# Moving the matmul operands of a hybrid decoder layer to other places in SBUF, modulo 512 bytes

## The chip, the core and the metric

The kernel runs on one core of one Trainium2 chip. The metric is the device time of one execution in microseconds (us); the kernel before takes 1278.26 us, the median of three runs between 1277.83 and 1278.36.

Five engines matter here: PE (TensorE, matrix products; its weight loads are a stream of their own, PEld), DVE (VectorE), ACT (ScalarE), POOL (GpSimd) and SP, which issues nearly all the transfers. A matmul has a stationary operand of 128x128 (the weights, loaded first) and a moving operand that is streamed past it; the sum lands in PSUM. SBUF is the on-chip memory from which both are read, and what is changed is where in it some of these operands lie.

## The reference

One decoder layer on 1024 tokens plus 16 meta tokens of width 1024, all in float32:

```python
h = layer_norm(concat([meta, x]), in_ln_g, in_ln_b)
z = h @ w_in + b_in                                  # 1024 -> 3840
q, k, v, c_in, gates = split(z)
y_attn = swa_sink_attention(q, k, v, sinks, rel_bias) @ w_attn_proj
c = c_val * sigmoid(c_gate)                          # c_in in two halves
c = silu(layer_norm(causal_dwconv(c, 31 taps)))
y_conv = c @ w_conv_proj
mixed = sigmoid(g_attn) * y_attn + sigmoid(g_conv) * y_conv
h = layer_norm(ALPHA * h + mixed @ w_out, ln1_g, ln1_b)
up = causal_dwconv(h @ ffn_w_up, 3 taps)             # 1024 -> 2 * 2816
u, g = split(up)
f = (gelu(g) * u) @ ffn_w_down                       # 2816 -> 1024
out = layer_norm(ALPHA * h + f, ln2_g, ln2_b)[:, 16:]
```

## The kernel before

Every float32 operand of a product is split into a rounded high part and the remainder (`hi`, `lo`), and a product is three matmuls: high by high, high by low, low by high. The stages follow each other on PE: input projection (z), attention, the two branch projections with the gates, the output projection, then the feed-forward layer as two large products, `up` (line 1476) and `down` (line 1609), which are more than half of the time.

**Up.** Both large products are done by a scheme with seven block products in place of eight (sums of blocks are formed beforehand, results are combined afterwards). The layer's normalised rows are turned and stored as four blocks; seven sums or blocks of them (`B11, B21, BT2, BT1, BT3, BT4, B22`), each with its `hi` and `lo`, stay in SBUF for the whole product. They are held twice, once for each half of the tokens: sub 0 has 258 columns, sub 1 has 256. `B_AT[sub][q]` gives tile and column at which each lies. These are the moving operands. The stationary ones are blocks of the weights, in a ring of ten places (`RING`): four at the start of `RHO`, four in the buffers `whi`/`wlo` (called `ws` there), two more in `RHO` from column 6160. Weight block number n (seven for each of the 22 chunks c, in the order B11, B21, BT4, BT2, BT1, BT3, B22) goes to place n modulo 10.

For each chunk c, `prod` runs seven products in the order B11, B21, BT2, BT4, BT1, BT3, B22; each is twelve matmuls on sub 0 and then twelve on sub 1 with the same weights. That makes 154 products of twelve on each half. Within a product on sub 1 all twelve moving operands begin at the same address modulo 512 bytes, since 256 columns are 1024 bytes; on sub 0 they step by 8 bytes with k and by 32 between `hi` and `lo`. Behind PE, DVE and ACT combine the seven results, apply the three-tap convolution and the gelu, and split the weights that come next; SP loads the weights, stores the results and loads them again for `down`.

**Down.** `operand` loads 42 pairs of operands, splits them, and puts the i-th pair at `F_AT[i % 6]` (results of `up`, the stationary side here) and at `W_DN[i % 7]` (weights, the moving side, 512 columns). Five pairs in six have two rows of blocks and give 24 matmuls, the sixth has one and gives 12; the first pair of the second product is prepared ahead of the last one of the first. In all 924 matmuls.

**Where the tiles lie.** SBUF is given out by pools, from the left (low addresses up) and from the right (high addresses down), without gaps. The bytes per partition at which the tiles begin are, with the remainder modulo 512 in brackets: `whi`/`wlo`/`ws` 12736, 16832, 20928 and 25024 (448 each), `RHC` 53696 (448), `RHO` 86976 (448), `OA` 136672 (480), `RX` 187808 (416), `OC` 196064 (480). Columns have 4 bytes. `RHO` from column 6160 is therefore at 0, so that two of the ten ring places (8 and 9) are at 0 and the other eight at 448. The sums on sub 0 are at 448, 448, 480, 32, 96, 160, 416 in the order of `B_AT[0]`, on sub 1 four at 480 (`OC`) and three at 448 (`RHC`).

Besides these, `OC` holds the convolution branch and `OA` the attention branch as moving operands of the branch projections (tile `ps_p`), and `OA` (four of eight), `RX` and `RW` hold the weights, moving there, of the output projection (tile `ps_w`, lines 295 to 300). The order of the work is written out by hand for PE and in large part for DVE (`after` adds an order without a wait), the rest is left to a planner with ranks; a tile waits for those that held its bytes before.

Of the kernel before, what the change touches and what calls it, by code (L numbers as in the profile page):

```python
# [23 lines left out]
F = mybir.dt.float32  # L24
R = mybir.dt.float32r
# [4 lines left out]
P = 128  # L30
# [71 lines left out]
def tile_hybrid_layer(  # L102
# [41 lines left out]
    RHC = arena.tile([P, 8320], R, name="RHC")  # L144
    RHO = arena.tile([P, 8320], R, name="RHO")
# [745 lines left out]
    with rank(RK_EVAC):  # L891
# [8 lines left out]


    late = ctx.enter_context(tc.tile_pool(name="late", bufs=1, side="right", reuse_waits="tile"))
    OC = late.tile([P, 8320], R, name="OC")
    oa_stack = ExitStack()
    OA = oa_stack.enter_context(tc.tile_pool(name="oa", bufs=1, side="left", reuse_waits="tile")).tile(
        [P, 8320], R, name="OA")
    tmp_stack = ExitStack()
    tmp_p = tmp_stack.enter_context(tc.tile_pool(name="tmp", bufs=1, side="right", reuse_waits="tile"))

# [4 lines left out]
    def conv(c, hl, a, b):  # L914
        o = (c * 2 + hl) * T
        return OC[:, o + a:o + b]

    def pin(ins):

        if pinned:  # L920
            after(ins, pinned[-1])
        pinned.append(ins)
# [9 lines left out]
    def cln_var(g):  # L932
# [8 lines left out]

        hi, lo = (OC[:, i * T + a:i * T + b] for i in (2, 3))
        pin(dve.tensor_copy(hi, s_))
# [29 lines left out]
    def oo(r, hl, a, b):  # L973
        o = (r * 2 + hl) * T
        return OA[:, o + a:o + b]

# [38 lines left out]
    RX = rx_p.tile([P, 2064], R, name="RX")  # L1015
# [25 lines left out]
    def prep_wo(k, raw=None, behind=None):  # L1041
        if k < 4:
            hi, lo = OA[:, k * 2048:k * 2048 + 1024], OA[:, k * 2048 + 1024:k * 2048 + 2048]
        elif k < 6:
# [85 lines left out]
    def quadrant(sub, kk, h):  # L1130
        i = h * KC + kk * 4
        return FA[:, h1_at(sub, i):h1_at(sub, i + 4)]

    B_AT = [[(RHC, 6144), (RHO, 4096), (OA, 0), (OA, 2064), (OA, 4128), (OA, 6192), (RX, 0)],
            [(OC, 0), (OC, 2048), (OC, 4096), (OC, 6144), (RHC, 0), (RHC, 2048), (RHC, 4096)]]
    B11, B21, BT2, BT1, BT3, BT4, B22 = range(7)

    def bsum(sub, q, hl):
        n = SUB[sub][1] - SUB[sub][0]
        t, o = B_AT[sub][q]  # L1140
        return t[:, o + hl * 4 * n:o + (hl + 1) * 4 * n]
# [401 lines left out]
    T1, T3, T4, T2 = (blk(td, 0, 2048, q * 512) for q in range(4))  # L1543
    S2, S3, S4, S1 = (blk(sd, 0, 2048, q * 512) for q in range(4))

    F_AT = [(RHC, 6144), (RX, 0), (RHC, 2048), (RHO, 0), (RHO, 2048), (RHO, 4096)]
    W_DN = [(OC, 0), (OC, 2048), (OC, 4096), (OC, 6144), (RHC, 0), (RHC, 4096), (RHO, 6144)]

    RXFs = [RXF[:, 0:1024], RXF[:, 1024:2048]]
    FAs = [FA[:, i * 1024:(i + 1) * 1024] for i in range(6)]  # L1550
# [7 lines left out]
    def operand(i, src, j, n, raws, places):  # L1558
        raw = raws[i % len(raws)]
        if raw is None:  # L1560
            raw = wraw([P, D])
        raw = raw[:, :n * 512]
        ins = load(raw.rearrange("p (n c) -> p n c", c=512), src(j, n))
        after(ins, loads[-1] if loads else f_stores[-5])
        loads.append(ins)
        t, o = places[i % len(places)]
        hi, lo = (t[:, o + x:o + x + n * 512] for x in (0, 1024))
        nc.scalar.copy(hi, raw)
        los.append(nc.vector.tensor_tensor(lo, raw, f32(hi), OP.subtract))
        if len(los) > 1:  # L1570
            after(los[-1], evacs.pop() if evacs else los[-2])
        return hi, lo

    def down_operands():
# [4 lines left out]
        for i, (f, w, j, n) in enumerate(x):  # L1579
            yield (n,) + operand(i, f, j, n, F_RAW, F_AT) + operand(i, w, j, n, W_RAW, W_DN)  # L1580

# [181 lines left out]
```

## Time and profile before

| | |
|---|---|
| median of 3 runs | 1278.26 us (1277.83 to 1278.36) |
| the profiled execution | 1278.45 us |
| its span, first to last instruction | 1276.2 us |
| PE busy | 1265.2 us, 99% |
| PEld busy | 1192.4 us, 93% |
| DVE busy | 1084.1 us, 85% |
| ACT busy | 588.0 us, 46% |
| mean granted TensorE clock | 0.999 |
| up, line 1476 | from 612.3 to 1054.7 us of the span, 3696 matmuls |
| down, line 1609 | from 1054.7 to 1268.2 us, 924 matmuls |

The profile is one execution. Matmuls are pipelined: the record of one reaches past the start of the next, so that its length (280 ns for 256 columns in `up`) says little about the rate. The rate is read in the timeline, from the start of a row to the start of the row after it; a row there stands for a run of like matmuls, with its start, its length, the line, and the tiles as output<-moving,stationary. Tiles are named without numbers of buffers, so that `RHO` as weights can be any ring place in it; which one it is follows from the number of the weight block.

### The profile page before, as it was taken

The numbers are of one execution on the slowest core, as the hardware profiler recorded it, in microseconds if no ns is written. First come the engines' busy times: TensorE is split into PE (matmuls) and PEld (weight loads), VectorE is DVE, ScalarE is ACT, GpSimd is POOL, SyncE is SP. The second block draws the span as 40 slices with busy tenths as digits, with TensorE's granted clock in tenths as the row PEclk, the third lists the DMA queues.
The fourth block names the chain that finished last, engine by engine and source line by source line (L and its number), as shares of the span: only waits on it lengthen the run. The fifth ranks groups of instructions, "written<-read, shape, count | busy, mean of one in ns | idle before, by whom it ended". The sixth has DMA issues, their size and how long they took to land.

```text
span 1276.2 us, 21682 instructions
## 1 busy us (share of the span) xinstructions
PE 1265.2 (99%) x8546; PEld 1192.4 (93%) x8546; DVE 1084.1 (85%) x1837; ACT 588.0 (46%) x1066; POOL 53.0 (4%) x28
## 2 busy tenths in 40 slices
PE   9999999999999999999999999999999999999997
PEld 8999999999999999788899999999999998888886
DVE  7899989999998577548899898988989877995697
ACT  7523245645483223344755455455454544544330
POOL 0000000010112231000000000000000000000000
PEclk9999999999999999999999999999999999999999
DMA  7294633332256554222155545454454567998722
GB/s 275 73 306 108 181 94 100 100 95 88 67 149 191 156 150 117 83 99 81 53 169 195 185 176 201 163 202 149 157 191 161 200 226 280 389 328 297 247 83 83
DMA packets 96152, 212.10 MB, mean 166 GB/s; under 512 B 10787, under 2 KB 35939, under 8 KB 95922
## 3 DMA queue, kind: packets, MB, share of 16 engines
q1 hardware_dynamic: 84282, 199.64, 47.0%
q10 hardware_dynamic: 11768, 11.08, 2.7%
q8 instruction: 67, 1.10, 0.4%
q14 instruction: 35, 0.29, 0.1%
HBM read 150.29 MB, written 62.70 MB: 167 GB/s over the span
## 4 chain that ended last, share of the span: by engine, by line
PE 97%; DVE 1%; DMA 1%; ACT 0%; issue 0%; SPq 0%; DVEq 0%
PE px L1476 15%; PE py L1476 10%; PE ps_x L1609 9%; PE ps_z L299 8%; PE ps_z L295 8%; PE ps_z L300 8%; PE ps_z L1609 7%; PE pz L1476 5%; PE pw L1476 5%; PE ps_p L299 2%; PE ps_p L300 2%; PE ps_p L295 2%; PE ps_w L295 2%; PE ps_w L300 2%; PE ps_w L299 2%; PE ps_z L511 2%
## 5 line engine op out<-in xcount | busy, mean ns | idle before, releaser
L663 DVE SCALAR_TENSOR_TENSOR FA<-cin,cols,FA 128x1026 f32<-128x1026 f32 x120 | 155.1, 1304 | 0.2
L299 PE MATMUL ps_z<-RHC,whi 128*128 128x384 f32 (+2 forms) x324 | 104.7, 323 | 0.0
L295 PE MATMUL ps_z<-RHO,whi 128*128 128x384 f32 (+2 forms) x324 | 104.7, 323 | 0.0
L299 PE MATMUL ps_z<-RHO,whi 128*128 128x384 f32 (+2 forms) x324 | 104.0, 321 | 0.0
L295 PE MATMUL ps_z<-RHC,whi 128*128 128x384 f32 (+2 forms) x324 | 103.9, 321 | 0.0
L300 PE MATMUL ps_z<-RHC,wlo 128*128 128x384 f32 (+2 forms) x324 | 103.6, 320 | 0.0
L300 PE MATMUL ps_z<-RHO,wlo 128*128 128x384 f32 (+2 forms) x324 | 103.3, 319 | 0.0
L1298 DVE TENSOR_TENSOR RHO<-wr,RHO 128x512 fp32r<-128x512 f32 x94 | 63.4, 684 | 10.9 <-ACT RHO L1297 10.9
L1297 ACT CAST RHO<-wr 128x512 fp32r<-128x512 f32 x94 | 56.6, 619 | 21.3 <-DVE wr L1315 9.9
L266 ACT CAST whi<-wr 128x1024 fp32r<-128x1024 f32 x37 | 38.9, 1052 | 56.8 <-PE ps_z L299 34.3
L295 PEld LDWEIGHTS ps_z<-RHO,whi 128*128 128x128 f32 x324 | 60.9, 188 | 0.5 <-issue 0.3
L299 PEld LDWEIGHTS ps_z<-RHC,whi 128*128 128x128 f32 x324 | 60.9, 188 | 0.4
L300 PEld LDWEIGHTS ps_z<-RHC,wlo 128*128 128x128 f32 x324 | 61.0, 188 | 0.2
L300 PEld LDWEIGHTS ps_z<-RHO,wlo 128*128 128x128 f32 x324 | 60.9, 188 | 0.1
L295 PEld LDWEIGHTS ps_z<-RHC,whi 128*128 128x128 f32 x324 | 60.8, 188 | 0.2
L299 PEld LDWEIGHTS ps_z<-RHO,whi 128*128 128x128 f32 x324 | 60.9, 188 | 0.1
L1315 DVE TENSOR_TENSOR wr<-wr 128x512 f32<-128x512 f32 x88 | 60.0, 682 | 0.2
L1488 ACT COPY FA<-px 128x514 f32<-128x514 f32 (+2 forms) x23 | 13.1, 571 | 82.0 <-PE px L1476 82.0
L269 POOL TENSOR_TENSOR wlo<-wr,whi 128x1024 fp32r<-128x1024 f32 x17 | 41.3, 2429 | 187.4 <-ACT whi L266 168.9
L670 ACT ACTIVATE FA<-ps_z,cols 128x386 f32<-128x386 f32 (+2 forms) x48 | 26.0, 541 | 46.7 <-PE ps_z L300 42.2
L1298 DVE TENSOR_TENSOR ws<-wr,ws 128x512 fp32r<-128x512 f32 x60 | 40.6, 684 | 6.1 <-ACT ws L1297 6.0
L1476 PE MATMUL px<-OA,RHO 128*128 128x258 f32 x324 | 43.5, 283 | 0.0
(467 smaller groups left out, 3589.1 us busy)
## 6 DMA issues: line engine op xcount, KB each, us to landing
wr<-in_w_up_dram SPq DMA_DIRECT2D x44, 512.0 KB, 4.3
wr<-in_w_z_dram SPq DMA_DIRECT2D x30, 512.0 KB, 3.6
fd<-FA SPq DMA_DIRECT2D x44, 256.0 KB, 2.4
OB<-in_w_down_dram SPq DMA_DIRECT2D x19, 512.0 KB, 5.8
qt<-qd SPq DMA_DIRECT2D x28, 256.0 KB, 3.8
td<-OB SPq DMA_DIRECT2D x12, 512.0 KB, 3.2
sums<-fd SPq DMA_DIRECT2D x12, 512.0 KB
sd<-sums SPq DMA_DIRECT2D x12, 512.0 KB, 2.8
```

The costliest lines, as they stand in the source:

```text
L266: ins = nc.scalar.copy(hi, raw)
L269: return (nc.vector if quick else nc.gpsimd).tensor_tensor(lo, raw, f32(hi), OP.subtract)
L295: ins = nc.tensor.matmul(ps, ah, bh, start=i == 0, stop=False)
L299: nc.tensor.matmul(ps, ah, bl, start=False, stop=False)
L300: last = nc.tensor.matmul(ps, al, bh, start=False, stop=i == n - 1)
L663: nc.vector.scalar_tensor_tensor(acc[c], cin[:, j:j + U], wc, acc[c], OP.mult, OP.add)
L670: nc.scalar.activation(t, ps, AF.Tanh, bias=bcol(14 + i), scale=0.5)
L1297: nc.scalar.copy(hi, src)
L1298: ins = nc.vector.tensor_tensor(lo, src, f32(hi), OP.subtract)
L1315: ins = nc.vector.tensor_tensor(*x)
L1476: ins = nc.tensor.matmul(o, x[:, ks], bmat(sub, q, hl, k), start=first and k + j == 0, stop=k == 3 and j == 2, skip_group_check=not first)
L1609: nc.tensor.matmul(banks[i], l[:, ts], r[:, ws], start=first and a and x + k == 0, stop=z and x == len(ops) - 1 and k == 2, skip_group_che ...
```

## The change

Two small tiles that nothing reads or writes are added: 96 bytes in the pool of `OC`, 32 bytes in front of `OA`. `OC` comes to lie 96 bytes lower, at 195968 (384 modulo 512), and with it all that is given out below it on the right: `RX` to 187712 (320), `RW`, the raw and sum buffers of `down`. `OA` goes to 136704 (0). In `RHC` the operands of `up` and of `down` begin 112 columns, 448 bytes, later, which is 384 modulo 512. The sums on sub 0 come to 384, 448, 0, 64, 128, 192, 320, on sub 1 all seven to 384. In `down` the stationary side is at 384, 320, 384, 448, 448, 448, and the moving side at 384 six times and at 448 once. No instruction is added, removed or resized; the weights of `up` stay where they are.

```diff
     late = ctx.enter_context(tc.tile_pool(name="late", bufs=1, side="right", reuse_waits="tile"))
+
     OC = late.tile([P, 8320], R, name="OC")
+    late.tile([P, 24], F, name="pad_c")
     oa_stack = ExitStack()
-    OA = oa_stack.enter_context(tc.tile_pool(name="oa", bufs=1, side="left", reuse_waits="tile")).tile(
-        [P, 8320], R, name="OA")
+    oa_p = oa_stack.enter_context(tc.tile_pool(name="oa", bufs=1, side="left", reuse_waits="tile"))
+    oa_p.tile([P, 8], F, name="pad_a")
+    OA = oa_p.tile([P, 8320], R, name="OA")
...
-    B_AT = [[(RHC, 6144), (RHO, 4096), (OA, 0), (OA, 2064), (OA, 4128), (OA, 6192), (RX, 0)],
-            [(OC, 0), (OC, 2048), (OC, 4096), (OC, 6144), (RHC, 0), (RHC, 2048), (RHC, 4096)]]
+    B_AT = [[(RHC, 6256), (RHO, 4096), (OA, 0), (OA, 2064), (OA, 4128), (OA, 6192), (RX, 0)],
+            [(OC, 0), (OC, 2048), (OC, 4096), (OC, 6144), (RHC, 112), (RHC, 2160), (RHC, 4208)]]
...
-    F_AT = [(RHC, 6144), (RX, 0), (RHC, 2048), (RHO, 0), (RHO, 2048), (RHO, 4096)]
-    W_DN = [(OC, 0), (OC, 2048), (OC, 4096), (OC, 6144), (RHC, 0), (RHC, 4096), (RHO, 6144)]
+    F_AT = [(RHC, 6256), (RX, 0), (RHC, 2160), (RHO, 0), (RHO, 2048), (RHO, 4096)]
+    W_DN = [(OC, 0), (OC, 2048), (OC, 4096), (OC, 6144), (RHC, 112), (RHC, 4208), (RHO, 6144)]
```

## The prediction

> **What bounds the kernel now.** I read the page's first part, the chain, PE's waits, a table by stage, and then PE's timeline.
>
> ```profile
> PE 1265.2 (99%) x8546; PEld 1192.4 (93%) x8546; DVE 1084.1 (85%) x1837; ACT 588.0 (46%) x1066; POOL 53.0 (4%) x28
> PE 97%; DVE 1%; DMA 1%; ACT 0%; issue 0%; SPq 0%; DVEq 0%
> ```
>
> PE is the chain: 97% of the span hangs on it. So any nanosecond taken from or added to a matmul reaches the end, if nothing else becomes late.
>
> ```profile
> engine line waited for: us in total, times, longest us
> PE pw L1476 <- ACT FA L1278: 0.9, 1, 0.9
> PE px L1476 <- ACT OB L1488: 0.4, 1, 0.4
> ...
> core 0: us, PE busy (x) PEld busy (x) DVE busy (x) ACT busy (x) POOL busy (x), PEclk, DMA share, GB/s
> 740.00:850.00 110.00, 110.00 (x930) 110.00 (x929) 101.63 (x163) 55.17 (x93) 0.00 (x0) 1.00 0.52 182
> 1054.70:1150.00 95.30, 95.30 (x415) 77.29 (x414) 82.06 (x103) 42.85 (x45) 0.00 (x0) 1.00 0.92 332
> ```
>
> PE waits for nobody worth naming, and its clock is full (1.00). In `up` DVE is busy 101.63 of 110 us, 92%: a cover that would be gone if PE got more than 8% faster. In the first half of `down` the transfers are at 0.92 of the DMA engines; that one I come back to.
>
> What is left to change is thus how long one matmul takes. Rows of `up` on PE, from chunks 4, 7 and 8 (start, length, line, output<-moving,weights; I take start to start):
>
> ```profile
> 698.31 1.60 PE L1476 MATMUL pz<-RHO 128*128 128x258 f32 x12
> 699.75 1.58 PE L1476 MATMUL pz<-OC,RHO 128*128 128x256 f32 x12
> ...
> 761.06 1.60 PE L1476 MATMUL px<-OA,RHO 128*128 128x258 f32 x12
> 762.50 1.57 PE L1476 MATMUL px<-OC,RHO 128*128 128x256 f32 x12
> 763.90 1.61 PE L1476 MATMUL pw<-OA,RHO 128*128 128x258 f32 x12
> 765.35 1.59 PE L1476 MATMUL pw<-RHC,RHO 128*128 128x256 f32 x12
> 766.77 1.60 PE L1476 MATMUL py<-OA,RHO 128*128 128x258 f32 x12
> ...
> 773.92 1.59 PE L1476 MATMUL py<-RHC,ws 128*128 128x256 f32 x12
> 775.35 1.60 PE L1476 MATMUL px<-RHC,ws 128*128 128x258 f32 x12
> 776.79 1.57 PE L1476 MATMUL px<-OC,ws 128*128 128x256 f32 x12
> 778.20 1.59 PE L1476 MATMUL pz<-RHO,ws 128*128 128x258 f32 x12
> 779.62 1.57 PE L1476 MATMUL pz<-OC,ws 128*128 128x256 f32 x12
> 781.03 1.62 PE L1476 MATMUL px<-OA,RHO 128*128 128x258 f32 x12
> 782.49 1.58 PE L1476 MATMUL px<-OC,RHO 128*128 128x256 f32 x12
> 783.91 1.60 PE L1476 MATMUL pw<-OA,RHO 128*128 128x258 f32 x12
> 785.35 1.53 PE L1476 MATMUL pw<-RHC,RHO 128*128 128x256 f32 x12
> 786.71 1.61 PE L1476 MATMUL py<-OA,RHO 128*128 128x258 f32 x12
> ```
>
> The row to see is 785.35 against 765.35: the same product one chunk later, the same moving tile `RHC` at 448 modulo 512, 256 columns, twelve matmuls. One takes 1.42 us (765.35 to 766.77), the other 1.36 (785.35 to 786.71). The difference is the ring place of the weights: block 7x8+2 = 58 is in place 8, at 0 modulo 512, so that the moving operand lies 64 bytes below its weights; block 51 is in place 1, at 448, the same address. I call moving minus weights the distance d. On sub 1 the trace thus has: d = 0, 1.42 to 1.43 (765.35, 773.92); d = +32 (`OC` on 448), 1.40 to 1.41 (762.50, 776.79, 779.62); d = -32 (`OC` on place 9, block 59), 1.42 (782.49); d = -64, 1.36. The change puts all seven sums of sub 1 at 384, which is d = -64 for eight ring places of ten and d = -128 for two.
>
> **The change part by part.** Nothing is issued more or less, no queue is passed, and no wait is added in the code: the sums in `RHC` now straddle two of its old rows of `mixed`, but the last of these to be read, for the row tile before the first of the sums, is the same one as before. So the cost is in the rates alone.
>
> *Sub 1 of `up`.* Of 154 products 30 have their weights in places 8 and 9 (n modulo 10): 17 with `OC`, 13 with `RHC`. The other 124 go to d = -64: 71 from `OC` at 1.405 and 53 from `RHC` at 1.425. I take 1.365 for each, the row at 785.35 with half a hundredth for its rounding: 71 x 0.04 + 53 x 0.06 = 6.0 us less. The 30 go to d = -128, which the trace doesn't show; bounds 1.36 and 1.43, the fastest and slowest sub 1 rows. Now they take 17 x 1.42 + 13 x 1.36 = 41.8; at the bounds 40.8 or 42.9, so -1.0 to +1.1. Nothing puts it nearer to either; I take the middle, 0.
>
> *Sub 0 of `up`.* Here the distance steps within a product and the rows differ less: `OA` 1.44, 1.45, 1.46, 1.44 (761.06, 763.90, 781.03, 783.91), `RHC` 1.44 (775.35), `RHO` 1.42 and 1.44 (778.20, 698.31). `OA` is at odd multiples of 32 from the weights, `RHC` and `RHO` at a multiple of 64, and `OA` goes to multiples of 64. 132 products move (all but `RHO`'s 22): between 0.02 less and 0.02 more each, -2.6 to +2.6. The even rows are on average 0.014 below the odd ones, which over 88 `OA` products would be 1.2; with so few rows I take -0.5.
>
> *`down`.* Its rows, 24 matmuls of 512 columns each:
>
> ```profile
> 1054.67 5.76 PE L1609 MATMUL ps_z<-OC,RHC 128*128 128x512 f32 x24
> 1060.27 5.66 PE L1609 MATMUL ps_z<-OC,RX 128*128 128x512 f32 x24
> 1065.78 5.76 PE L1609 MATMUL ps_z<-OC,RHC 128*128 128x512 f32 x24
> ...
> 1076.97 5.63 PE L1609 MATMUL ps_z<-RHC,RHO 128*128 128x512 f32 x24
> 1082.44 2.88 PE L1609 MATMUL ps_z<-RHO,RHC 128*128 128x512 f32 x12
> 1085.16 5.61 PE L1609 MATMUL ps_x<-RHC,RHO 128*128 128x512 f32 x24
> 1090.61 5.65 PE L1609 MATMUL ps_x<-OC,RX 128*128 128x512 f32 x24
> ...
> 1115.65 5.61 PE L1609 MATMUL ps_z<-RHC 128*128 128x512 f32 x24
> 1121.09 5.75 PE L1609 MATMUL ps_z<-RHO,RX 128*128 128x512 f32 x24
> 1126.69 5.77 PE L1609 MATMUL ps_z<-OC,RHC 128*128 128x512 f32 x24
> ```
>
> d = +32 takes 5.60 (1054.67, 1121.09), d = +64 5.51 (1060.27), d = 0 5.44 to 5.47 (1115.65, 1076.97, 1085.16), say 5.45. Walking i through `F_AT[i % 6]` and `W_DN[i % 7]` gives, in units of 24 matmuls: before, 21 at +32, 13.5 at 0, 4 at +64, in sum 117.6 + 73.6 + 22.0 = 213.2 us (the stage is 213.5). After: 14.5 at 0, 7.5 at +64, 1 at +128, and 15.5 at d = -64, which 512 columns don't show. Its bounds: 5.60, the slowest row, and 5.33, which is d = 0 less what the same step saves on 256 columns (0.06 on twelve). d = 0 and d = +64, the nearest multiples of 64, stand at 5.45 and 5.51; I take 5.50. After: 79.0 + 41.3 + 5.5 + 85.3 = 211.1, so -2.1, with bounds -4.8 and -0.6.
>
> *Output and branch projections.*
>
> ```profile
> 534.86 0.40 PE L295 MATMUL ps_w<-OA,RHC 128*128 128x512 f32 x1
> ...
> 536.96 0.40 PE L295 MATMUL ps_w<-OA,RHC 128*128 128x512 f32 x1
> ```
>
> Nine matmuls with `OA` take 2.10 us, 233 ns each, as `down`'s d = +32. Four of eight weight rows are in `OA`; 192 matmuls (8 row tiles x 2 halves x 4 x 3) go from +32 to +64, 5.60 to 5.51 on 24: -0.7. `RX` and `RW` go from -32 to -128, and the branch projections' 768 matmuls from odd to even multiples of 32: 0, give or take 1.
>
> Sum: -6.0 + 0 - 0.5 - 2.1 - 0.7 = -9.3. Against the profiled execution, 1278.45 us (span 1276.2 and 2.3 around it, 0.2 above the median), that is 1269.1, and about 1269 against the median.
>
> **What may become late.** In `up` a chunk of 20.0 us (762.50 to 782.49 is one) gets 0.3 shorter; DVE's 92% becomes 94%, still covered. In `down` the tight place is here:
>
> ```profile
> 1081.09 0.69 DVE L1569 TENSOR_TENSOR RHO<-OB,RHO 128x512 fp32r<-128x512 f32 x1 [0.52 <-ACT RHO L1568]
> ...
> 1088.07 1.23 DVE L1569 TENSOR_TENSOR OC<-OB,OC 128x1024 fp32r<-128x1024 f32 x1
> ```
>
> The last pair of the first product is ready at 1081.78 and used at 1082.44: 0.66 us to spare. It hangs on the last chunk's result, stored and loaded again, so it moves with the end of `up`, but not with PE's own gain in that product: pairs at d = 0, +64, 0, -64, -64 make 27.4 in place of 27.77, a gain of 0.36 that still fits; at 5.33 it is 0.70 and just doesn't. The second product has 1.3 (1089.30 to 1090.61). A loss here can't exceed the gain, under 1 us.
>
> [...]
>
> **The rivals.** *No change:* the 1.36 belongs to ring places 8 and 9 themselves and not to the distance. For: both kinds of address differ between the two rows, and only one pair at d = -64 exists. Against: `OC` on place 9 takes 1.42, slower than on the others, so the place alone doesn't make it fast. Then sub 1 stays at 1.40 to 1.43 and the other terms make 0 to -3: 1277 (1275.5 to 1278.5). [...]
>
> *Slower:* the pair at 384 with weights at 448 collides worse than any now. For: on sub 0 d = -64 is not fast (698.31 to 699.75: the `RHO` sums on place 9, block 29, take 1.44, more than the 1.42 of `RHO` on place 7 at 778.20), and a rate jumps by 4% over 32 bytes (1.36 at -64, 1.42 at -32) in a way that I can't model. Price: all 154 sub 1 products at 1.45, the slow sub 0 rows' rate, are 223.3 in place of 217.1, +6.2; `down` at 5.60 -0.6: 1284. It decides from where a sub 1 product takes 1.43 on average: there its loss eats the 3.3 us of the other terms.
>
> *Larger gain:* d = -64 is a floor for all widths: `down` -4.8, the 30 products -1.0, sub 0 -1.5, beside -6.0 and -0.7: 14.0 less, some 0.3 lost at the tight place: 1264.7.
>
> **How the numbers follow.** Chances: the forecast 0.58 (own range 1266 to 1273), larger 0.17, no change 0.13, slower 0.12. The measurement can tell about 0.2%, 2.6 us: faster takes the first two and a little of the third, 0.77; within it 0.11; slower 0.12. For 8 in 10 I leave out the slower case and the far end of the large one: 1263.5 to 1278.5.
>
> **What would show it.** In PE's timeline: sub 1 rows with `OC` and `RHC` at 1.36 to 1.37 start to start, except those with weights in places 8 and 9; a chunk at 19.7; `up` 435.9 long in place of 442.4; `down` at 211; PE without waits. Wrong if sub 1 rows stay at 1.40 or above, or if `down` rows with `OC` on `RHO` are not below 5.60.

## The result and the profile after

The changed kernel takes 1274.70 us, the median of 9 runs (1274.20 to 1275.54), beside 1278.22 us of the kernel before on the same chip (9 runs, 1277.83 to 1278.77): a ratio of 0.9973 [0.9965, 0.9981], 3.5 us or 0.28% less. The direction was forecast; of the 9.3 us forecast little more than a third came. The time lies inside the range on record, and outside the likeliest case's own range of 1266 to 1273.

The page's first part and its chain, for the kernel after, whose span is 1273.1 us (before 1276.2):

```profile
PE 1261.4 (99%) x8546; PEld 1189.6 (93%) x8546; DVE 1084.0 (85%) x1837; ACT 587.9 (46%) x1066; POOL 53.1 (4%) x28
PE 96%; DMA 2%; DVE 1%; ACT 0%; issue 0%; SPq 0%; DVEq 0%; ACTq 0%
```

PE is still the chain, and the busy times of DVE, ACT and POOL moved by 0.1 us at most. PE's waits in `up` (engine, bank and line, what it waited for: us, times, longest):

```profile
PE pw L1480 <- ACT FA L1282: 1.0, 1, 1.0
PE px L1480 <- ACT OB L1492: 0.5, 1, 0.5
```

They are the two of before, each 0.1 us longer. Ahead of `up` one wait of 0.5 us on a transfer is new (in the attention stage), but `up` begins where it did. The gain that is missing, 5.8 us, was not given back in waits, which are 0.7 us longer in all; it was never in the matmuls. The table by stretch, for the whole of `up`, of the kernel before and of the one after (stretch, length, busy time of PE, PEld, DVE, ACT and POOL, clock, DMA share, GB/s):

```profile
612.30:1054.70 442.40, 441.06 (x3706) 440.19 (x3705) 397.93 (x637) 233.36 (x388) 0.00 (x0) 1.00 0.50 177
```

```profile
612.20:1051.80 439.60, 438.10 (x3705) 437.27 (x3704) 397.83 (x637) 232.99 (x388) 0.00 (x0) 1.00 0.50 177
```

`up` begins at the same place and is 2.8 us shorter; the forecast was 6.5. `down` takes 212.9 us from its first to its last matmul in place of 213.2; the forecast was 2.1 less. PE's timeline of the kernel after, a chunk all of whose weights are in ring places 0 to 7, so that every sub 1 product is at d = -64 (start, length, then the instruction; the rate is from one start to the next):

```profile
818.22 1.52 PE L1480 MATMUL pz<-OC,RHO 128*128 128x256 f32 x12
819.58 1.60 PE L1480 MATMUL px<-OA,RHO 128*128 128x258 f32 x12
821.01 1.52 PE L1480 MATMUL px<-OC,RHO 128*128 128x256 f32 x12
822.37 1.63 PE L1480 MATMUL pw<-OA,RHO 128*128 128x258 f32 x12
823.84 1.53 PE L1480 MATMUL pw<-RHC,RHO 128*128 128x256 f32 x12
825.21 1.61 PE L1480 MATMUL py<-OA,ws 128*128 128x258 f32 x12
826.66 1.54 PE L1480 MATMUL py<-OC,ws 128*128 128x256 f32 x12
828.04 1.60 PE L1480 MATMUL px<-OA,ws 128*128 128x258 f32 x12
829.47 1.58 PE L1480 MATMUL px<-RHC,ws 128*128 128x256 f32 x12
830.89 1.62 PE L1480 MATMUL py<-RX,ws 128*128 128x258 f32 x12
832.34 1.53 PE L1480 MATMUL py<-RHC,ws 128*128 128x256 f32 x12
833.71 1.60 PE L1480 MATMUL px<-RHC,ws 128*128 128x258 f32 x12
835.14 1.58 PE L1480 MATMUL px<-OC,ws 128*128 128x256 f32 x12
```

The 256-column rows are what to look at. All have the same distance, and they do not have the same rate: `B21` (818.22), `BT2`, `BT4`, `BT1` and `B22` take 1.36 to 1.38, but `BT3` (829.47 to 830.89) takes 1.42, and so does `B11` (835.14; its next start is 836.56). Matmul by matmul, the medians over the chunks show two steady rates (the first chunk, which runs its seven sub 1 products one after another and ahead of its sub 0 ones, is left out of medians here and below): 113 ns in the fast products from the fourth matmul on at the latest, 117.5 ns in `B11` and `BT3` to the end. Nothing lies between. Weights in ring places 8 and 9 (d = -128) give 1.42 to 1.44.

All start-to-start times of sub 1, without the few real gaps: the 124 products with weights in places 0 to 7 went from 1.415 on average to 1.386, which is -3.7 us in place of the -6.0 forecast; the 30 with places 8 and 9 from 1.399 to 1.425, +0.8 in place of 0. Sub 0 stays at 221.8 us in sum.

In `down` the same view gives:

```profile
1057.31 5.66 PE L1613 MATMUL ps_z<-OC,RX 128*128 128x512 f32 x24
1062.80 5.60 PE L1613 MATMUL ps_z<-OC,RHC 128*128 128x512 f32 x24
1068.24 5.76 PE L1613 MATMUL ps_z<-OC,RHO 128*128 128x512 f32 x24
1073.84 5.76 PE L1613 MATMUL ps_z<-RHC,RHO 128*128 128x512 f32 x24
```

`OC` on `RX` (d = +64) takes 5.49, `OC` on `RHC` (d = 0) 5.44, and `OC` and `RHC` on `RHO`, now at d = -64, 5.60 (1079.44 is the start after 1073.84): exactly what d = +32 took before. Over all of `down` a matmul takes 233.3 ns at d = -64, 230.1 at +64 (384 on 320) and 227.8 at 0.

### The profile page after: what moved, and what is told of

Read it like the earlier page. It is cut to its first block, busy times and chain, and to the rows that moved or that the text cites. A ratio compares the mean times of both kernels' runs of the same rounds, so it can differ in the third digit from the quotient of the medians.

```text
span 1273.1 us, 21682 instructions
## 1 busy us (share of the span) xinstructions
PE 1261.4 (99%) x8546; PEld 1189.6 (93%) x8546; DVE 1084.0 (85%) x1837; ACT 587.9 (46%) x1066; POOL 53.1 (4%) x28
## 4 chain that ended last, share of the span: by engine, by line
PE 96%; DMA 2%; DVE 1%; ACT 0%; issue 0%; SPq 0%; DVEq 0%; ACTq 0%
PE px L1480 15%; PE ps_x L1613 10%; PE py L1480 10%; PE ps_z L299 7%; PE ps_z L295 7%; PE ps_z L300 7%; PE ps_z L1613 7%; PE pz L1480 5%; PE pw L1480 5%; PE ps_p L299 2%; PE ps_p L300 2%; PE ps_p L295 2%; PE ps_w L300 2%; PE ps_w L295 2%; PE ps_w L299 2%; PE ps_z L511 2%
```

## The experiments

The theory from these rows: the rate hangs on the distance d, but a distance does not have one rate. At -64 with 256 columns there are two that last (113 and 117.5 ns), and what comes just before decides which one a product falls into; with 512 columns -64 is simply a slow distance (233.3 ns against 227.8 at 0). The rivals: the place of the tiles and not the distance; the PSUM bank (`B11` and `BT3` both write `px`) or the copies of ACT and DVE behind it; contention that passes with time.

**The last two ring places at 448 too.** Only the two weight places at 0 are moved, so that all 154 sub 1 products are at d = -64.

```diff
-    RING += [RHO[:, 6160 + i * 1024:6160 + (i + 1) * 1024] for i in range(2)]
+    RING += [RHO[:, 6272 + i * 1024:6272 + (i + 1) * 1024] for i in range(2)]
```

> The changed kernel, with the two ring places that lie at 0 modulo 512 moved to 448, so that every sub 1 product has its moving operand 64 bytes below its weights. If the distance sets the rate, the 30 products with those weights, now at 1.42 to 1.44 us at a distance of -128, go to 1.36 to 1.42, and the time from 1274.7 to about 1273.3. If the place of the weights sets it, or if every distance but the ones seen is as good, they stay at 1.42 to 1.44 and the time at 1274.7.

Measured: 1272.77 us (1272.63 to 1273.12), ratio 0.9958 [0.9943, 0.9973]; `up` 438.0. The chunk with weight blocks 58 and 59, which used places 8 and 9, in the timeline of this kernel:

```profile
780.14 1.52 PE L1480 MATMUL px<-OC,RHO 128*128 128x256 f32 x12
781.50 1.63 PE L1480 MATMUL pw<-OA,RHO 128*128 128x258 f32 x12
782.97 1.53 PE L1480 MATMUL pw<-RHC,RHO 128*128 128x256 f32 x12
784.34 1.61 PE L1480 MATMUL py<-OA,RHO 128*128 128x258 f32 x12
```

`BT2` with block 59 takes 1.36, `BT4` with block 58 takes 1.37, as with any other ring place. Before, place 8 with `RHC` was the one fast row; it is fast at 448 as well, once the moving operand is 64 bytes below. So it is the distance and not the place, and the rival of the place falls. `B11` and `BT3` stay at 1.416 in all chunks.

**Two sums on sub 0 exchanged.** `BT4` and `BT3` swap their places in `OA` on sub 0. On sub 1 nothing is touched: same addresses, same banks, same copies behind them.

```diff
-    B_AT = [[(RHC, 6256), (RHO, 4096), (OA, 0), (OA, 2064), (OA, 4128), (OA, 6192), (RX, 0)],
+    B_AT = [[(RHC, 6256), (RHO, 4096), (OA, 0), (OA, 2064), (OA, 6192), (OA, 4128), (RX, 0)],
```

> The changed kernel, with the sub 0 sums of BT3 and BT4 exchanged in OA; the sub 1 sums, the weights and the PSUM banks stay. Theory: at a distance of -64 a run of matmuls has two lasting rates, 113 and 117.5 ns, and the sub 0 product just ahead of it decides which one it falls into; the sums at 128 modulo 512 lead into the slow one. Then BT4's sub 1 products (bank pw) go from 1.37 to 1.416 us and BT3's (bank px) from 1.416 to 1.36 to 1.38, time 1274.7 within 1. Rival: the bank px, or the copies by ACT that read it, make its products slow. Then BT3 stays at 1.416 and BT4 at 1.37.

Measured: 1274.36 us (1274.0 to 1275.2), ratio 0.9971 [0.9960, 0.9983]. The same chunk as above, `BT4` and `BT3` on sub 1, each with the start after it:

```profile
822.88 1.58 PE L1480 MATMUL pw<-RHC,RHO 128*128 128x256 f32 x12
824.30 1.62 PE L1480 MATMUL py<-OA,ws 128*128 128x258 f32 x12
...
828.59 1.53 PE L1480 MATMUL px<-RHC,ws 128*128 128x256 f32 x12
829.96 1.61 PE L1480 MATMUL py<-RX,ws 128*128 128x258 f32 x12
```

`BT4` now takes 1.42 (before this edit 823.84 to 825.21, 1.37), `BT3` 1.37 (1.42). The slow rate followed the sub 0 operand that precedes it, from bank `px` to `pw`. That settles the bank and the copies: neither decides. The operand that makes the next product slow is in both kernels the one at d = 192 on sub 0 (or, for `B11`, at -64, the same modulo 256); the distance of a sub 0 product is given as that of its first operand.

**`down` at a distance of 0.** Three places of `F_AT` and one of `W_DN`, all in `RHO`, move to 384; 756 matmuls are then at d = 0, the other 168 at +64.

```diff
-    F_AT = [(RHC, 6256), (RX, 0), (RHC, 2160), (RHO, 0), (RHO, 2048), (RHO, 4096)]
-    W_DN = [(OC, 0), (OC, 2048), (OC, 4096), (OC, 6144), (RHC, 112), (RHC, 4208), (RHO, 6144)]
+    F_AT = [(RHC, 6256), (RX, 0), (RHC, 2160), (RHO, 112), (RHO, 2160), (RHO, 4208)]
+    W_DN = [(OC, 0), (OC, 2048), (OC, 4096), (OC, 6144), (RHC, 112), (RHC, 4208), (RHO, 6256)]
```

> The changed kernel, with down's operands in RHO moved by 112 columns to 384 modulo 512, where its other moving operands lie: 756 of 924 matmuls at a distance of 0, 168 at +64, none at -64. If the distance 0 is what makes 227 ns at 512 columns, down goes from 212.9 us to 756 x 227.6 + 168 x 230.1 = 210.7, the time to 1272.5. If the rate belongs to the absolute place (448), or to what is run before it, it stays near 233 and the time at 1274.7.

Measured: 1271.37 us (1270.87 to 1271.84), ratio 0.9947 [0.9932, 0.9962]; `down` 209.65 in place of 212.88. The rows of the timeline that were at d = -64:

```profile
1066.98 5.60 PE L1613 MATMUL ps_z<-OC,RHO 128*128 128x512 f32 x24
1072.42 2.88 PE L1613 MATMUL ps_z<-RHC,RHO 128*128 128x512 f32 x12
```

They take 5.44 in place of 5.60. Both operands are at 384 here; in the kernel before, with both at 448, d = 0 took 5.44 to 5.47 as well, so here too it is not the place. On 512 columns d = 0 is the fast distance (5.44 us on 24 matmuls, 5.60 at -64), and on 256 it is -64 (1.36 us on twelve, 1.42 to 1.43 at 0 in the kernel before): neither of the two offsets is the faster one in both stages. The median gain over the changed kernel, 3.3 us, is that of the stage, 3.2.

**`B11` with another operand in front.** On sub 0 `B11` moves to d = 0 and leaves d = -64; three sums on sub 1 and four places of `down` (two of `F_AT` and two of `W_DN`, not shown here) shift to make room, at unchanged remainders.

```diff
-    B_AT = [[(RHC, 6256), (RHO, 4096), (OA, 0), (OA, 2064), (OA, 4128), (OA, 6192), (RX, 0)],
-            [(OC, 0), (OC, 2048), (OC, 4096), (OC, 6144), (RHC, 112), (RHC, 2160), (RHC, 4208)]]
+    B_AT = [[(RHC, 0), (RHO, 4096), (OA, 0), (OA, 2064), (OA, 4128), (OA, 6192), (RX, 0)],
+            [(OC, 0), (OC, 2048), (OC, 4096), (OC, 6144), (RHC, 2160), (RHC, 4208), (RHC, 6256)]]
```

> The changed kernel, with B11's sub 0 sum at the start of RHC (448, a distance of 0) and the three sub 1 sums behind it, still at 384; down's operands follow, still at 384. By the theory of the two rates the sub 0 product at a distance of 0 leads into the fast one, as it does for B21: B11's sub 1 products go from 1.416 to 1.36 us and its sub 0 products from 1.433 to 1.418, 17 x 0.056 + 18 x 0.015 = 1.2 less, 1273.5. If the bank px makes the product slow, only the sub 0 part comes, 1274.4.

Measured: 1275.30 us (1274.73 to 1275.73), ratio 0.9977 [0.9968, 0.9987]: a miss, no gain over the changed kernel. `B11` and `B21` in the timeline of this kernel:

```profile
812.99 1.63 PE L1480 MATMUL px<-RHC,RHO 128*128 128x258 f32 x12
814.46 1.53 PE L1480 MATMUL px<-OC,RHO 128*128 128x256 f32 x12
815.83 1.63 PE L1480 MATMUL pz<-RHO 128*128 128x258 f32 x12
817.30 1.53 PE L1480 MATMUL pz<-OC,RHO 128*128 128x256 f32 x12
```

The step under test came true: `B11` on sub 1 takes 1.37 in place of 1.42. But the two sub 0 products at d = 0 take 1.47, while `B21` at that same distance took 1.418 in the changed kernel. There the product in front, `B11` on sub 1, ran at the slow rate; here it runs at the fast one. So the entry works in both directions here: behind a fast sub 1 product (1.37) a sub 0 product at d = 0 takes 1.47, behind a slow one (1.416) 1.418. The changed kernel had shown this already, in a product that the expectation left out: `BT4`, at -256 and so at 0 modulo 256, takes 1.468 there behind a fast `BT2`. Without the gaps, sub 1 gained 0.5 us and sub 0 lost 1.3.

**Matmuls alone.** No other engine works beside PE; weights and moving tile lie at the same address modulo 512, and the moving operand starts i x 32 bytes later, i from 0 to 15 and back, each distance for 36 matmuls of 256 columns, then the same with 24 matmuls of 512.

```python
for n, count in ((256, 36), (512, 24)):
    for i in list(range(16)) + list(range(15, -1, -1)):
        run(i, n, count, "r")      # moving M[:, i*8 : i*8+n]
```

> Matmuls alone, with rows of x as both operands and none of the layer's work: one block of weights after another at one address modulo 512, and the moving operand at 16 distances from it, 32 bytes apart, first with rising and then with falling distance; 36 matmuls at each with 256 columns, then 24 with 512. By the distance theory 256 columns last at about 120 ns at a distance of 0, 117 at +32, and either 113 or 117.5 at -64, and 512 columns at 227 at 0, 230 at +64, 233 at +32 and at -64, whatever the absolute place. By the theory of two lasting rates some distance comes out differently on the way up and on the way down. If the rates belong to the traffic of the other engines, all distances come out alike here.

Measured (349.97 us, one run; in its span of 348.2 us ACT is busy for 2.8, DVE for 0.7 and POOL for 0.2), steady start-to-start ns of one matmul on the way up (means without the last step and without the first twelve at 256 columns, the first eight at 512):

| d modulo 256 | 0 | 32 | 64 | 96 | 128 | 160 | 192 (= -64) | 224 (= -32) |
|---|---|---|---|---|---|---|---|---|
| 256 columns | 120.0 | 117.8 | 117.8 | 120.2 | 118.9 | 117.4 | 113.3 | 118.4 |
| 512 columns | 226.7 | 233.3 | 228.9 | 233.3 | 233.6 | 234.3 | 233.3 | 233.2 |

The second eight distances repeat the first eight within 0.2 ns: on the way up the pattern has a period of 256 bytes. Of these distances -64 alone is fast on 256 columns (113.3, the others 117.4 to 120.2); on 512 it is 0 (226.7), then 64 (228.9), and -64 (233.3) is as slow as the odd multiples of 32 (233.2 to 234.3). With 256 columns some rows differ on the way back. The largest difference is at d = 192, entered from 160 on the way up and from 224 on the way back (timeline, `psg` is i = 6).

```profile
45.30 4.28 PE L45 MATMUL psg<-M,W 128*128 128x256 f32 x36
49.41 4.42 PE L45 MATMUL psh<-M,W 128*128 128x256 f32 x36
...
125.84 4.40 PE L45 MATMUL psg<-M,W 128*128 128x256 f32 x36
130.08 4.43 PE L45 MATMUL psf<-M,W 128*128 128x256 f32 x36
```

The same 36 instructions take 4.11 us from start to start on the way up and 4.24 on the way back, 113.3 against 117.8 ns, to the last of them. But the other d = 192 on the way back (i = 14, 91.90 to 96.01), entered from 224 too, is fast at 113.3. Two more distances differ by over 1 ns: 32 takes 116.6 and 116.7 on the way back (117.8 and 117.7 on the way up), and 160 once takes 118.6 (117.4).

**Entry alone.** Again matmuls only: 24 at an entry distance, 0 to 224 in steps of 32, then 48 at d = -64, the whole twice.

```python
for i in list(range(8)) * 2:
    run(i, 256, 24, "e")           # entry distance i*32
    run(14, 256, 48, "r")          # d = -64
```

> Matmuls alone, none of the layer's work: 256 moving columns, weights and moving tile at the same address modulo 512. Sixteen times 24 matmuls at an entry distance (0, 32, 64 up to 224 bytes, twice over) and then 48 matmuls at d = -64. Theory of two lasting rates that the entry decides: each stretch of 48 keeps one rate, 113.3 or 117.8 ns per matmul, to its end, which differs between stretches although the 48 are the same instructions with the same addresses; both rates occur. Rival, that the slower rate in the layer comes from the work of the other engines beside it: no other engine works here, so all sixteen stretches run at 113.3. Rival, that the slower rate decays in time: it falls to 113.3 within the 48.

The timeline, stretches entered from 96 (46.58) and from 128 (54.89):

```profile
46.58 5.62 PE L45 MATMUL psg<-M,W 128*128 128x256 f32 x48
52.04 3.01 PE L45 MATMUL pse<-M,W 128*128 128x256 f32 x24
54.89 5.82 PE L45 MATMUL psg<-M,W 128*128 128x256 f32 x48
60.54 3.01 PE L45 MATMUL psf<-M,W 128*128 128x256 f32 x24
```

48 equal matmuls take 5.46 us or 5.65. Entered from 0, 32, 64, 96 and 224 they settle at 113.3 to 113.4 ns within six matmuls; from 128, 160 and 192 at 117.7 to 117.8 until the last one. The second pass gives the same for all eight. With no other engine at work, that rules out contention from DVE, ACT and the transfers as a needed cause, and the rate doesn't decay in 48 matmuls. The entry from 160 came out slow here and fast in the run before, where 160 itself had another history (117.4 ns against 118.7 here): the last distance alone doesn't determine it. Nor do these entries carry over to the layer. Alone, the entry from 32 leads into the fast rate (113.3 to 113.4 ns), those from 128 and 160 into the slow one (117.7 to 117.8). In the layer a sub 0 product at 128 (`BT1` in the changed kernel, 1.376 us on sub 1) or at 160 (`BT3` with `OA` back at 480, below, 1.363) leads into the fast rate, and one at 32 (`BT2` there, 1.416) into the slow one. A sub 0 product has no single distance, since its operands step by 8 and by 32 bytes; whether that is the reason was not tested.

**All of it together.** The ring at 448, `down` and the output projection at d = 0 throughout, and as many sub 0 sums as there is room for at d = 64, the entry after which sub 1 had been fast (`BT2` in the changed kernel, 1.36 us). The edits to the ring (as above), to the sizes of `RX` and `RW` and to the places of the output projection's weights are not shown.

```diff
-    B_AT = [[(RHC, 6256), (RHO, 4096), (OA, 0), (OA, 2064), (OA, 4128), (OA, 6192), (RX, 0)],
-            [(OC, 0), (OC, 2048), (OC, 4096), (OC, 6144), (RHC, 112), (RHC, 2160), (RHC, 4208)]]
+    B_AT = [[(RHC, 16), (RHO, 4112), (OA, 0), (OA, 6256), (OA, 2064), (OA, 4128), (RX, 32)],
+            [(OC, 0), (OC, 2048), (OC, 4096), (OC, 6144), (RHC, 2160), (RHC, 4208), (RHC, 6256)]]
...
-    F_AT = [(RHC, 6256), (RX, 0), (RHC, 2160), (RHO, 0), (RHO, 2048), (RHO, 4096)]
-    W_DN = [(OC, 0), (OC, 2048), (OC, 4096), (OC, 6144), (RHC, 112), (RHC, 4208), (RHO, 6144)]
+    F_AT = [(RHC, 112), (RX, 0), (RHC, 4208), (RHO, 112), (RHO, 2160), (RHO, 4208)]
+    W_DN = [(OC, 0), (OC, 2048), (OC, 4096), (OC, 6144), (RHC, 2160), (RHC, 6256), (RHO, 6256)]
```

> A layout made from the rows of the runs before: all ring places at 448; sub 1 at a distance of -64; sub 0 at +64, +64, +64, +192, 0, +128, +64 in the order of work; down all at 0; the output projection's weights in OA, RX and RW at 0. From the rows: sub 0 and sub 1 together 2.793 us for a +64 product, 2.849 and then 2.778 for +192 followed by 0, 2.824 for +128, so 19.62 us a chunk against 19.95 in the changed kernel, 22 x 0.33 = 7.2 less; down 209.7 against 212.9; output projection 288 matmuls at 227 in place of 230 to 233, about 1 to 2 less: 1274.7 - 7.2 - 3.2 - 1.5 = 1262.8. If the rate that a sub 0 product takes hangs on what is ahead of it as much as on its distance, the chunk comes out between 19.62 and 19.95, and the time at up to 1270.

Measured: 1265.74 us (1265.35 to 1266.40), ratio 0.9905 [0.9889, 0.9922]; 2.9 above what was expected. The rows came as expected, a chunk of 19.63 at the median against 19.62. What was wrong is the chunk it was compared with: the changed kernel's is 19.83 and not 19.95, which is about that of the kernel before (19.96). So `up` gains 22 x 0.20 = 4.4 and not 7.2; it is at 435.5, 4.1 less than in the changed kernel. `down` is at 209.2. One sub 1 product of seven is still slow, `BT4` (819.97 to 821.38 here), behind its sub 0 operand, which this layout puts at d = 192:

```profile
818.54 1.60 PE L1480 MATMUL pw<-OA,RHO 128*128 128x258 f32 x12
819.97 1.58 PE L1480 MATMUL pw<-RHC,RHO 128*128 128x256 f32 x12
821.38 1.58 PE L1480 MATMUL py<-OA,ws 128*128 128x258 f32 x12
```

**`OA` back at 480.** The changed kernel without the 32 bytes ahead of `OA`.

```diff
-    oa_p.tile([P, 8], F, name="pad_a")
```

> The changed kernel without the 32 bytes in front of OA: four sub 0 sums are at odd multiples of 32 from the weights again, as before the change, all else as changed. If OA's move was worth something of its own, by which sub 0 products at multiples of 64 are cheaper and lead into the fast rate, it costs 1 to 3 us, 1275.5 to 1277.5. If sub 0 doesn't matter to sub 1, the rows of sub 0 go back to what they were and the time stays at 1274.7 within 0.7.

Measured: 1275.41 us (1274.98 to 1275.96), ratio 0.9979 [0.9970, 0.9989]: 0.7 above the changed kernel, with ranges that overlap, so the time alone decides nothing. The rows do: on sub 1 `BT2` (its sub 0 operand is at d = 32 here) goes from 1.359 to 1.416 (820.85 to 822.26 in this kernel's timeline), and `BT3` (160) from 1.416 to 1.363. So sub 0 does matter to sub 1, but as many products become slow as become fast. Sub 0 itself stays at 221.8 us, so multiples of 64 are not cheaper there, and `up` is 439.4, 0.2 shorter than with `OA` moved. The 192 matmuls of the output projection with `OA` take 233.4 ns (230.0 in the changed kernel), 0.65 us in sum; but `up` starts at 612.2 in both profiled executions, so it is not shown that this makes the 0.7.

**Three sums on sub 0 off the bad entries.** Made from the table of all rows so far, on the combined layout; the rates expected of `BT4` and `BT3` are those of their rows in the run with `OA` back at 480.

```diff
-    B_AT = [[(RHC, 16), (RHO, 4112), (OA, 0), (OA, 6256), (OA, 2064), (OA, 4128), (RX, 32)],
+    B_AT = [[(RHC, 16), (RHO, 4112), (OA, 0), (OA, 6208), (OA, 2072), (OA, 4136), (RX, 32)],
```

> The layout with the ring at 448, down at d = 0 (1265.74 us), but three sums on sub 0 moved within OA: BT4 from d = 192 to 224, BT3 from 128 to 160, BT1 from 0 to -192. If a distance counts modulo 256 and a product's two rates can be read from a table of the runs so far: BT4 1.446 then 1.362 (in place of 1.432 then 1.416), BT3 1.443 then 1.363 (1.451, 1.376), BT1 as +64, 1.434 then 1.360 (1.418, 1.360): 46 ns less on each of 21 chunks, 1.0 us: 1264.8. If what comes before the product also counts, one of the three misses its pair of rates, by up to 0.06 us, and the time lies between 1264.5 and 1267.

Measured: 1264.47 us (1264.16 to 1264.73), ratio 0.9894 [0.9877, 0.9910], the fastest of all. Its page begins:

```profile
PE 1250.4 (99%) x8546; PEld 1183.4 (94%) x8546; DVE 1083.9 (86%) x1837; ACT 588.6 (47%) x1066; POOL 53.2 (4%) x28
```

A chunk of its timeline, from `BT4` on sub 0 on:

```profile
818.10 1.61 PE L1480 MATMUL pw<-OA,RHO 128*128 128x258 f32 x12
819.55 1.52 PE L1480 MATMUL pw<-RHC,RHO 128*128 128x256 f32 x12
820.91 1.59 PE L1480 MATMUL py<-OA,ws 128*128 128x258 f32 x12
822.35 1.52 PE L1480 MATMUL py<-OC,ws 128*128 128x256 f32 x12
823.70 1.60 PE L1480 MATMUL px<-OA,ws 128*128 128x258 f32 x12
825.15 1.53 PE L1480 MATMUL px<-RHC,ws 128*128 128x256 f32 x12
826.51 1.59 PE L1480 MATMUL py<-RX,ws 128*128 128x258 f32 x12
```

`BT4` takes 1.45 and 1.36, `BT1` 1.44 and 1.35, `BT3` 1.45 and 1.36; the medians over 21 chunks are 1.445 and 1.362, 1.434 and 1.359, 1.443 and 1.364, each within 0.001 of the expectation. All sub 1 products behind the first chunk settle at 113 ns, `up` is 434.4, and DVE is still in time: PE's list of waits names 1.0 us in `up`, where the changed kernel had 1.5.

## Why the prediction was right in direction and wrong in size

Two terms of the sum failed, and both for the same reason: a rate at d = -64 was taken from too little. On 256 columns one row stood for all 124 products, -6.0 us forecast and -3.7 measured; on 512 columns, where no row showed d = -64, the choice of 5.50 us gave -2.1, and 5.60 with -0.3 was measured. That the time lies in the range on record says little, since the range is 15 us wide and holds no change as well.

*That the rates are the whole of it:* right. PE stayed the chain (96%), its waits in `up` stayed (1.5 us, before 1.3), and DVE kept up, even at a chunk of 19.6 us (809.72 to 829.30 in the last kernel).

*The distance and not the place:* right. The rival "no change" as the prediction put it, that the 1.36 belongs to places 8 and 9, fell with the ring run. Nor is the address of no account: nothing but addresses was changed, and the kernels with the same instructions run from 1264.47 to 1278.22 us. The two rates, 113.3 and 117.8 ns, came with no other engine at work as well.

*Sub 1 at d = -64, "1.365 for each":* the sign was right and the term mis-sized, -3.7 us in place of -6.0. The step took one row (785.35) for the rate of a distance. Five products of seven did get that rate; `B11` and `BT3` fell into the second lasting rate of 1.416, because of the sub 0 operand in front of them (1.37 with another one there, in the exchange and in the run that moved `B11`). 34 products x 0.05 are 1.7 of the 2.3 us; the rest is that `BT4` and `BT1` take 1.372 and 1.376, that seven of the 20 products next after one with its weights in place 8 or 9 take 1.41 to 1.42 where the same sums elsewhere take 1.36 to 1.38 (`B21` and `BT1` twice each, `BT2` three times), and that in the first chunk `B21` takes 1.41 and `BT4` 1.49. The prediction's test "sub 1 rows stay at 1.40 or above" thus came out split, by product.

*The 30 products at d = -128, "the middle, 0":* +0.8, inside the bounds of -1.0 to +1.1 and near the bad one.

*Sub 0, -0.5:* 0. The reading behind it, that even multiples of 32 are cheaper, did not hold: of the four products with `OA`, `BT4` went from 1.447 to 1.468 and `BT1` from 1.434 to 1.451, `BT2` from 1.430 to 1.434, and only `BT3` fell, from 1.442 to 1.433 (places 0 to 7). The sum stayed.

*`down`, "I take 5.50" at d = -64:* wrong. It is 5.60, the upper bound, so the term is -0.3 and not -2.1. The choice of the value by "the nearest multiples of 64", 0 and +64, was the failing step: with 512 columns 64 below is not like 64 above (233.3 against 228.9 ns in the run of matmuls alone), and what is fast on 256 columns is not on 512. The prediction named this sign (rows of `OC` on `RHO` not below 5.60) as what would make it wrong. Even the bound of -0.6 at 5.60 was 0.3 too good, because d = +64 takes 230.1 ns on average, 5.52 on 24, and d = 0 5.47.

*Output projection, -0.7:* its own rows gave 0.65, from 233.4 to 230.0 ns on 192 matmuls. It can't be seen at the start of `up` (612.3 and 612.2 us): kernels that are alike up to there start it anywhere from 611.3 to 612.2.

The terms as measured, -3.7, +0.8, 0 and -0.3, make -3.2, and with the 0.1 us by which `up` starts earlier -3.3; the span fell by 3.1, the median by 3.5.

What stays open: why there are two lasting rates, and what in the entry picks one. The runs show that an operand's distance modulo 256 (113.3 to 120.2 ns on 256 columns) and the rate in front of it (1.418 or 1.468 us for d = 0 on sub 0) both count; no run here shows the mechanism behind it, and no table of entries holds both for the matmuls alone and for the layer.

## What to carry to other kernels

When PE is the whole chain, lay out operands by measured rates: time the same matmul alone at all distances between moving and stationary address modulo 256, for each width that the kernel uses, since here the best distance of one width (-64 at 256 columns, 113.3 ns) was a bad one at another (512: 233.3 against 226.7 at 0). The rates found so were within 1.5 ns those of the layer (113.3 alone and 113 there at -64 on 256 columns, 226.7 and 227.8 at 0 on 512, 228.9 and 230.1 at 64), but what leads into which of two rates had to be read in the kernel itself (128 led into 117.7 to 117.8 ns alone and into 113 in the layer). One fast row is not the rate of its distance (1.36 in the row, 1.386 on average over the 124 products); look at every product with that distance, and at what runs in front of it, before multiplying. Then move the operand that spoils the entry, and expect the product after it to change as well (1.418 to 1.47 us here). Take the time that a new layout is compared with from the rows of the kernel it is measured against: 19.95 us a chunk in place of 19.83 made one expectation here 2.8 us too good.

## What the runs showed of the hardware that was not expected

- Matmuls with equal operands, equal addresses and no other engine at work have two rates that last, 113.3 and 117.8 ns on 256 columns at d = -64, and what PE ran before decides between them (48 matmuls, the same outcome in both passes); the distance just before does not alone decide (in the run with 16 distances 224 led into both).
- In the layer sub 0 depends on the rate in front too: at d = 0 the `B21` product takes 1.418 us behind a slow product and 1.47 behind a fast one, where `BT4` takes 1.468.
- In the run of matmuls alone the distance counts modulo 256 bytes: 0 and 256, 64 and 320, 192 and 448 agree within 0.2 ns on 512 columns. On that width a matmul takes 226.7 ns at 0, 228.9 at 64, and 233 to 234 at the other multiples of 32.
- Placement alone, with not one instruction added or removed, was worth 13.6 us of 1278.1, 1.1%.
